# One access pattern over both directions in the HGRN2 levels, and 24 modulation vectors computed in halves inside attention: two-layer hybrid diffusion backbone

## The chip, the cores and the metric

The kernel runs on one core of one Trainium2 chip. The metric is the device time of one execution in microseconds (us). Engines are named as in the profile: PE is TensorE (PEld its weight loads), DVE is VectorE, ACT is ScalarE, POOL is GpSimd, SP is SyncE, whose queue issues the DMAs.

## The reference

One inference step of two post-norm layers over 1152 tokens (1024 latent, 128 context) of width 1024, all in float32. In each layer the stream is scaled and shifted by modulation vectors, `mod = silu(cvec) @ w_mod + b_mod` (6 x 1024 columns, for two condition vectors), projected once, and split among three mixers: latent attention with 8 heads, a bidirectional mLSTM, and a bidirectional gated linear recurrence (HGRN2). Their outputs are joined, projected, gated and normalised; a modulated SwiGLU FFN follows. The part of the recurrence that matters here, per direction, with `lb` the layer's lower bound (zero in layer 0):

```python
def decay(fr):
    f = lb + (1.0 - lb) * jax.nn.sigmoid(fr)
    return (1.0 - lb) * jax.nn.sigmoid(-fr), jnp.log(jnp.maximum(f, TINY))
...
Bc = jnp.cumsum(gc, axis=2)
decay = jnp.exp(Bc[:, :, :, None, :] - Bc[:, :, None, :, :])
A = jnp.einsum('bhtsc,bhsc->bhts', qc[:, :, :, None, :] * decay, kc)
```

## The kernel before

Products of float32 precision are made of three matmuls on pairs of rounded high and low parts (`mm3`, L153). The code is written in program order; a list scheduler that works at build time orders each engine's instructions by their dependencies and this order, so the order on the chip is not that of the source, and an engine works through its queue strictly in the order that was fixed.

Each layer has four phases. Phase A (`phase_a`, L367) computes the projections for HGRN2 and the mLSTM, and the inputs of attention, which it spills to memory. HGRN2 goes in two halves p of two heads each: `project` (three units: two gates, query), then the column group gi, during which `prep` (L521) turns the gates into cumulative logarithms, then the groups ckv and cq in `mla_prep` (L883), then `states` and, for each of three blocks b of 384 tokens, `outs` (L588). `outs` builds the token-by-token matrix A of three chunks of 128 tokens: a diagonal product, evicted by DVE with a multiplication by the identity (L600), and seven levels with block sizes m = 64 to 1. A level takes four differences on POOL (L610 to L613, forward and backward halves apart, 192 columns each), one exponential on ACT, three products on DVE (L615 to L617), six matmuls, and two masked copies by DVE into A (L624). L645 copies the output of a chunk. There are 2 layers x 2 halves x 3 blocks x 7 = 84 levels. The mLSTM (`mlstm`, L811) ends phase A; in layer 0 its normalising products run on POOL, in layer 1 on DVE (`LG`, L816).

Phase B is attention (`phase_b`, L965). After the projections of head 0 it goes through 152 steps (8 heads x 19 blocks of keys and queries). A step issues the score matmuls, the exponential on ACT (L1185), its rounding on ACT (L1186), the subtraction that gives the low part on POOL (L1187), and the product with the values of the step two before. Into the steps generators are mixed, two pieces per step: the maxima of the next head's scores (L1136 on PE, L1137 on DVE), projections of later heads, and at the end `rec` (L1222), which gates the recurrent outputs. DVE's other work from two SBUF tiles there is L1108, L151 and the copies of L1128. Phase C is the output projection with the first normalisation, phase D the FFN.

Of the 48 x 128 modulation columns layer 0 needs sixteen blocks ("vectors") at the start; the others are computed beside other work by `mod_gemv` (L209): a load of 512 KB and two dot products on DVE (L213), one per condition vector. Vectors 16 to 23 run in gi, ckv and cq, 24 to 39 in the mLSTM (`start_mod`, L282: two load buffers, its own copies cB of the conditions), 40 to 47 in the FFN's input, and those of layer 1 in the FFN's output (L1620), three per token tile of its first two passes. `gsave` (L222) transposes the gate vectors on PE and stores them. A branch for vectors in attention exists (L1283 to L1292) but starts at 40 and does nothing.

## Time and profile before

| | us |
|---|---|
| median of 3 runs | 3641.23 (3634.70 to 3644.34) |
| the profiled execution | 3641.28 |
| its span, first to last instruction | 3639.5 |
| mean granted clock of TensorE | 0.953 of 2.4 GHz |

Layer 0 runs from 0 to about 1795 us: phase A to about 560, attention's steps from 614.6 to 933.3, the FFN's output from 1542. Layer 1 fills the rest, attention's steps from 2394.6 to 2707.8. Busy time of PE is modelled and overstates its rate; stages are best compared by the times between like instructions of the two layers, which do the same work but for the vectors and the place of `LG`.

### The profile page before, as it was taken

How to read it: one execution, taken by the hardware profiler on the slowest of the kernel's cores; microseconds unless marked ns; L12 is line 12 of the kernel's file. 1: busy time of each engine (PE TensorE's matmuls, PEld its weight loads, DVE VectorE, ACT ScalarE, POOL GpSimd, SP SyncE). 2: the span in 40 equal slices, each digit the busy share in tenths (PEclk: the TensorE clock that was granted, in tenths of full speed). 3: DMA queues.
4: the chain of work that ended last, by engine and by line, in shares of the span. 5: the costliest groups of instructions: out<-in, count | busy, mean ns of one | idle time of the engine just before them, and what ended most of it. 6: DMA issues, size and time to landing. Idle time of an engine off the chain costs nothing. (4 is left out here: it accounts for less than half of the span.)

```text
span 3639.5 us, 56085 instructions
## 1 busy us (share of the span) xinstructions
PE 3405.9 (94%) x20556; PEld 3034.6 (83%) x20556; DVE 2264.8 (62%) x4492; ACT 1635.7 (45%) x2877; POOL 1988.8 (55%) x1745
## 2 busy tenths in 40 slices
PE   7999987999989999999889989989999999999997
PEld 7998875776779999988689888877767899998875
DVE  6868878555674444487775678765558544443246
ACT  4264564887343333312272636577853433333211
POOL 3455566777665555401453556567863555552176
PEclk9899976999989999999999999789999999999998
DMA  6212153002352222375422021401044322224222
GB/s 244 72 40 43 39 167 100 18 21 81 121 160 85 85 85 85 111 252 179 156 79 62 30 45 34 137 25 25 22 132 139 110 73 73 73 74 139 94 99 80
DMA packets 331272, 335.77 MB, mean 92 GB/s; under 512 B 191458, under 2 KB 270386, under 8 KB 330996
## 3 DMA queue, kind: packets, MB, share of 16 engines
q1 hardware_dynamic: 330996, 332.19, 29.5%
q8 instruction: 161, 2.64, 0.3%
q14 instruction: 115, 0.94, 0.1%
HBM read 263.54 MB, written 68.56 MB: 91 GB/s over the span
## 5 line engine op out<-in xcount | busy, mean ns | idle before, releaser
L151 POOL TENSOR_TENSOR t<-t,t 128x512 fp32r<-128x512 f32 (+3 forms) x318 | 437.8, 1378 | 374.8 <-ACT t L150 374.4
L150 ACT CAST t<-t 128x512 fp32r<-128x512 f32 (+5 forms) x404 | 270.7, 673 | 698.0 <-PE bank L1449 278.7
L1449 PE MATMUL bank<-hhi,t 128*128 128x256 f32 (+1 forms) x2816 | 570.8, 295 | 12.4 <-DVE t L1349 11.5
L155 PE MATMUL bank<-hhi,t 128*128 128x384 f32 (+1 forms) x1220 | 455.1, 378 | 19.2 <-ACT t L150 5.1
L157 PE MATMUL bank<-hhi,t 128*128 128x384 f32 (+1 forms) x1220 | 460.0, 378 | 8.8 <-DVE t L151 8.8
L1449 PEld LDWEIGHTS bank<-hhi,t 128*128 128x128 f32 x2816 | 456.2, 189 | 13.6 <-ACT t L150 12.3
L156 PE MATMUL bank<-hlo,t 128*128 128x384 f32 (+1 forms) x1220 | 460.9, 378 | 4.9 <-POOL hlo L151 4.1
L1187 POOL TENSOR_TENSOR t<-t,t 128x512 fp32r<-128x512 f32 (+1 forms) x304 | 383.3, 1281 | 125.4 <-ACT t L1186 103.0
L1449 PE MATMUL bank<-t,t 128*128 128x320 f32 (+1 forms) x3168 | 434.2, 297 | 2.3 <-DVE t L1507 1.7
L1449 PEld LDWEIGHTS bank<-t,t 128*128 128x128 f32 x3168 | 427.9, 190 | 3.7 <-DVE t L1507 1.9
L1449 PE MATMUL bank<-hlo,t 128*128 128x320 f32 (+1 forms) x1408 | 415.2, 295 | 0.0
L155 PE MATMUL bank<-t,hhi 128*128 128x256 f32 (+3 forms) x1232 | 386.8, 315 | 12.1 <-DVE t L1107 5.4
L156 PE MATMUL bank<-t,hhi 128*128 128x256 f32 (+3 forms) x1232 | 388.0, 315 | 4.3 <-POOL t L146 4.3
L157 PE MATMUL bank<-t,hlo 128*128 128x256 f32 (+3 forms) x1232 | 388.4, 316 | 0.3 <-POOL hlo L151 0.3
L155 PEld LDWEIGHTS bank<-hhi,t 128*128 128x128 f32 x1220 | 237.9, 196 | 57.3 <-ACT t L150 6.7
L1137 DVE TENSOR_REDUCE t<-bank 128x1 f32<-128x384 f32 (+1 forms) x400 | 203.9, 538 | 122.6 <-PE bank L1136 119.5
L157 PEld LDWEIGHTS bank<-hhi,t 128*128 128x128 f32 x1220 | 240.1, 197 | 39.2 <-DVE t L151 12.1
L156 PEld LDWEIGHTS bank<-hlo,t 128*128 128x128 f32 x1220 | 239.6, 196 | 34.7 <-POOL hlo L151 5.1
L1449 PEld LDWEIGHTS bank<-hlo,t 128*128 128x128 f32 x1408 | 265.4, 188 | 0.3 <-issue 0.2
L155 PEld LDWEIGHTS bank<-t,hhi 128*128 128x128 f32 x1232 | 239.8, 195 | 30.2 <-DVE t L1107 5.6
L213 DVE SCALAR_TENSOR_TENSOR t<-t,t 128x1024 bf16<-128x1024 f32 x176 | 239.3, 1359 | 40.6 <-DMA t<-in_w_mod_dram 31.6
L156 PEld LDWEIGHTS bank<-t,hhi 128*128 128x128 f32 x1232 | 240.4, 195 | 20.1 <-POOL t L146 4.7
(355 smaller groups left out, 7329.1 us busy)
## 6 DMA issues: line engine op xcount, KB each, us to landing
t<-in_w_mod_dram SPq DMA_DIRECT2D x96, 512.0 KB
t<-in_w_ffn_in_dram SPq DMA_DIRECT2D x88, 512.0 KB
t<-in_w_ffn_out_dram SPq DMA_DIRECT2D x44, 512.0 KB
t<-in_w_in_dram SPq DMA_DIRECT2D x40, 512.0 KB
shid<-t SPq DMA_DIRECT2D x88, 160.0 KB
sx<-t SPq DMA_DIRECT2D x27, 512.0 KB
t<-sx SPq DMA_DIRECT2D x27, 512.0 KB
shid<-t SPq DMA_DIRECT2D x88, 128.0 KB
```

Source lines behind the costliest of these rows:

```text
L150: self.nc.scalar.copy(hi, src)
L151: (eng or self.nc.gpsimd).tensor_tensor(lo, src, hi.bitcast(F32), op=ALU.subtract)
L155: mm(ps, a[0], b[0], start=first, stop=False)
L156: mm(ps, a[0], b[1], start=False, stop=False)
L157: mm(ps, a[1], b[0], start=False, stop=last)
L213: nc.vector.scalar_tensor_tensor(junk, raw, 1.0, cB[s], op0=ALU.mult, op1=ALU.mult, accum_out=self.modfm[:, l, j, s:s + 1])
L1137: V.tensor_reduce(nm[:, i, b:b + 1] if i < 8 else nm[:, i, 3:4], ps, axis=AX.X, op=ALU.max, negate=True)
L1187: G.tensor_tensor(pl, e, ph.bitcast(F32), op=ALU.subtract)
L1449: mm(ps, a[x][:, k * P:(k + 1) * P], view(y, k, n0, n1), start=first and k == 0 and i == 0, stop=k == 3 and i == 2, skip_group_check=True)
```

## The change

1. The five buffers of an HGRN2 half become two, `kq` (forward keys, backward keys, queries) and `bb` (both cumulative logarithms), so that one pattern reaches forward and backward halves: a level takes two POOL differences and two DVE products of 384 columns.
2. The diagonal product comes after the levels, by a masked copy with the identity as mask. The coarsest level is copied whole by ACT; the finer levels and the diagonal overwrite what does not belong to it.
3. `prep` leaves out the scaling by 1 - lb and the bound in layer 0, where lb is zero.
4. `start_mod` is gone. Vectors 16 to 39 are computed in layer 0's attention, one dot at three of every seven steps, with one load buffer `rv`; `cB` is loaded at the first step, and the buffers of `rec` lie in its storage.

```diff
+        def tiles(z):
+            kq, bb = z([P, 3, T]), z([P, 2, T])
+            return [kq[:, 2], kq[:, 0], kq[:, 1], bb[:, 0], bb[:, 1], kq, bb]
+
+        def halves(a, off, sh, nb, m, bcast=False):
+            return bass.AP(tensor=a.tensor, offset=a.offset + off, ap=[list(a.ap[0]), [2 * m, nb], [sh, 2], [0 if bcast else 1, m]])
...
-                    V.tensor_scalar(k[:, c], k[:, c], oml[:, p:p + 1], None, op0=ALU.mult)
-                    V.tensor_scalar(s, B[:, c], oml[:, p:p + 1], lb[:, p:p + 1], op0=ALU.mult, op1=ALU.add)
-                    V.tensor_scalar(s, s, TINY, None, op0=ALU.max)
+                    if l == 0:
+                        V.tensor_scalar(s, B[:, c], TINY, None, op0=ALU.max)
+                    else:
...
-                G.tensor_tensor(XS[:, :, 0, :], rf, F[:, :, 0, :], op=ALU.subtract)
-                G.tensor_tensor(XS[:, :, 1, :], rb, Bk[:, :, 1, :], op=ALU.subtract)
-                G.tensor_tensor(XM[:, :, 1, :], F[:, :, 1, :], rf, op=ALU.subtract)
-                G.tensor_tensor(XM[:, :, 0, :], Bk[:, :, 0, :], rb, op=ALU.subtract)
+                G.tensor_tensor(XS, halves(bb, o + m - 1, T + 1, nb, m, True), halves(bb, o, T + m, nb, m), op=ALU.subtract)
+                G.tensor_tensor(XM, halves(bb, o + T, m - T, nb, m), halves(bb, o + T + m, -T - 1, nb, m, True), op=ALU.subtract)
                 nc.scalar.activation(X, X, AF.Exp)
-                V.tensor_tensor(XS[:, :, 0, :], XS[:, :, 0, :], vw(kf[:, c])[:, :, 0, :], op=ALU.mult)
-                V.tensor_tensor(XS[:, :, 1, :], XS[:, :, 1, :], vw(kb[:, c])[:, :, 1, :], op=ALU.mult)
+                V.tensor_tensor(XS, XS, halves(kq, o, T + m, nb, m), op=ALU.mult)
                 V.tensor_tensor(X[:, 1, :], X[:, 1, :], q[:, c], op=ALU.mult)
+                product(X[:, 0], X[:, 1], (lambda o, ps: nc.scalar.copy(o, ps)) if li == 0 else pick(lmask[:, li, :]))
+            X = rX.next()
+            nc.gpsimd.tensor_tensor(X[:, 0, :], kf[:, c], kb[:, c], op=ALU.add)
+            product(X[:, 0], q[:, c], pick(imask))
...
-                        bg = self.start_mod(Zone(self, c, "gemv"), 16, 24) if l == 0 else iter(())
+                        bg = iter(())
...
-                bg = self.start_mod(zl, 24, 40) if l == 0 else iter(())
+                bg = iter(())
...
-            rdn = z.ring(2, [1, QB])
-            rr, rg = z.ring(3, [P, 256]), z.ring(3, [P, 256])
+            dn = z([33, QB])
+            rdn = Ring([dn[0:1, :], dn[32:33, :]])
+            cB = [z([P, D]) for _ in range(2)]
+            rr, rg = [Ring([a[:, 256 * i:256 * (i + 1)] for i in range(4)]) for a in cB]
+            if l == 0:
+                rv = z([P, U])
...
-            todo, gj = [], [40]
+            todo, mods = [], [(j, i) for j in range(16, 40) for i in range(2)]
...
+                if l == 0 and n == 0:
                     self.mod_init(cB)
+                if l == 0 and n % 7 in (0, 2, 4) and mods:
+                    j, i = mods.pop(0)
+                    if i == 0:
+                        nc.sync.dma_start(rv, ins["w_mod"][0, j])
+                    self.mod_dot(0, j, i, cB, rv, junk)
+                    if i == 1 and j % 8 == 7:
                         self.mod_bias(0, j - 7, 8)
+                    if (j, i) == (23, 1):
+                        self.gsave(0, 16, r_p.next())
```

`product` is the six matmuls and two evictions of a level as before, `pick` the masked copy, `mod_dot` one dot of `mod_gemv`.

## Rows read from the trace of the kernel before

**Rows 1.** The page, part 1: busy us, share of the span, instructions, by engine.
```profile
PE 3405.9 (94%) x20556; PEld 3034.6 (83%) x20556; DVE 2264.8 (62%) x4492; ACT 1635.7 (45%) x2877; POOL 1988.8 (55%) x1745
```

**Rows 2.** One line's instructions, layer 0, then 1: ns min/median/max; first, last start; forms.
```profile
L399 DVE TENSOR_TENSOR t<-bank,t x9: 392/413/415, 96.6 to 125.9; 128x256 f32<-128x256 f32 x9
...
L949 DVE TENSOR_TENSOR t<-bank,t x9: 393/416/425, 164.2 to 186.9; 128x256 f32<-128x256 f32 x9
...
L645 ACT COPY t<-bank x18: 247/266/281, 239.9 to 481.4; 128x128 f32<-128x128 f32 x18
...
L1185 ACT ACTIVATE t<-bank x152: 267/598/621, 614.6 to 926.8; 128x512 f32<-128x512 f32 x144, 128x128 f32<-128x128 f32 x8
...
L399 DVE TENSOR_TENSOR t<-bank,t x9: 400/425/425, 1910.0 to 1927.9; 128x256 f32<-128x256 f32 x9
...
L949 DVE TENSOR_TENSOR t<-bank,t x9: 391/417/419, 1959.8 to 1983.1; 128x256 f32<-128x256 f32 x9
...
L645 ACT COPY t<-bank x18: 247/266/279, 2040.0 to 2287.3; 128x128 f32<-128x128 f32 x18
...
L1185 ACT ACTIVATE t<-bank x152: 269/598/644, 2394.6 to 2702.0; 128x512 f32<-128x512 f32 x144, 128x128 f32<-128x128 f32 x8
```

**Rows 3.** Windows: length; busy us of PE, PEld, DVE, ACT, POOL; PEclk, DMA share, GB/s.
```profile
96.00:164.00 68.00, 62.06 (x478) 60.80 (x478) 59.65 (x171) 21.40 (x33) 33.47 (x31) 0.89 0.18 56
150.00:330.00 180.00, 178.76 (x1322) 168.06 (x1322) 135.28 (x362) 88.05 (x121) 96.95 (x122) 1.00 0.14 43
481.00:615.00 134.00, 96.23 (x456) 80.84 (x455) 121.14 (x329) 53.76 (x122) 94.86 (x96) 0.68 0.50 157
1985.00:2140.00 155.00, 145.19 (x1023) 135.12 (x1021) 107.97 (x257) 87.55 (x116) 83.28 (x111) 0.98 0.12 37
2287.00:2395.00 108.00, 90.40 (x457) 79.86 (x457) 91.32 (x294) 59.93 (x145) 55.10 (x65) 0.68 0.41 122
```

**Rows 4.** Line 213, the modulation dots, in 90 to 615 us: columns as rows 2.
```profile
L213 DVE SCALAR_TENSOR_TENSOR t<-t,t x44: 1198/1216/2010, 90.0 to 607.7; 128x1024 bf16<-128x1024 f32 x44
```

**Rows 5.** Lines of the HGRN part, whole span: columns as rows 2.
```profile
L593 POOL TENSOR_TENSOR t<-t,t x12: 1004/1020/1907, 83.6 to 2232.3; 128x384 f32<-128x384 f32 x12
...
L610 POOL TENSOR_TENSOR t<-t x84: 501/510/2485, 96.4 to 2272.7; 128x192 f32<-128x192 f32 x84
...
L615 DVE TENSOR_TENSOR t<-t,t x84: 293/359/2272, 107.5 to 2279.6; 128x192 f32<-128x192 f32 x84
...
L617 DVE TENSOR_TENSOR t<-t,t x84: 533/551/2724, 108.1 to 2280.2; 128x384 f32<-128x384 f32 x84
...
L527 DVE TENSOR_SCALAR t<-t,t x24: 405/420/2496, 79.4 to 2035.3; 128x384 f32<-128x384 f32 x24
```

**Rows 6.** Timeline 1110 to 1116 us, DVE, then POOL: start us, us, instruction, idle before.
```profile
1111.87 1.23 DVE L213 SCALAR_TENSOR_TENSOR t<-t,t 128x1024 bf16<-128x1024 f32 x1 [2.94 <-DMA t<-in_w_mod_dram]
...
1113.13 2.19 DVE L213 SCALAR_TENSOR_TENSOR t<-t,t 128x1024 bf16<-128x1024 f32 x1
...
1109.57 1.29 POOL L151 TENSOR_TENSOR t<-t,t 128x512 fp32r<-128x512 f32 x1 [1.20 <-ACT t L150]
1112.69 1.55 POOL L151 TENSOR_TENSOR t<-t,t 128x512 fp32r<-128x512 f32 x1 [1.83 <-ACT t L150]
```

**Rows 7.** Window of layer 0's first 109 attention steps: columns as rows 3.
```profile
614.00:841.00 227.00, 221.05 (x1075) 173.55 (x1075) 125.73 (x249) 186.58 (x364) 167.64 (x138) 0.98 0.08 17
```

**Rows 8.** Groups on DVE in 614 to 841: count, busy us, mean ns, idle before.
```profile
L1128 DVE CAST t<-hlo 32x1152 fp32r<-32x1152 f32 x5 | 6.8, 1355 | 1.0 <-PE bank L1182 0.8
L1108 DVE TENSOR_TENSOR t<-t,t 128x384 f32<-128x384 f32 x3 | 5.8, 1934 | 0.0
L151 DVE TENSOR_TENSOR t<-t,t 64x1152 fp32r<-64x1152 f32 x3 | 5.3, 1765 | 1.2 <-ACT t L150 1.1
```

**Rows 9.** Line 1611, evictions of the FFN output's first pass, layer 0, then 1.
```profile
L1611 ACT COPY t<-bank x18: 571/584/592, 1563.6 to 1662.8; 128x512 f32<-128x512 f32 x18
...
L1611 ACT COPY t<-bank x18: 572/586/589, 3340.5 to 3439.8; 128x512 f32<-128x512 f32 x18
```

More of the change, by code (lines that the diff above doesn't have):

```diff
@@ L390, in phase_a @@
                     zs = Zone(self, c0, f"hs{l}", "right")
-                    set0 = [zs([P, T]) for _ in range(5)]
+                    set0 = g.tiles(zs)
                     self.mark(f"hg{l}")
@@ L407, in phase_a @@
                     zt = Zone(self, cH, f"ht{l}")
-                    set1 = [zt([P, T]) for _ in range(5)]
+                    set1 = g.tiles(zt)
                     g.states(0, set0, v, rW)
@@ L487, in evac_unit @@
         def evac_unit(p, j, tiles):
-            q, kf, kb, Bf, Bb = tiles
+            q, kf, kb, Bf, Bb, kq, bb = tiles
             u = 3 * p + j
@@ L521, in prep @@
         def prep(p, tiles, rW):
-            q, kf, kb, Bf, Bb = tiles
+            q, kf, kb, Bf, Bb, kq, bb = tiles
             for b in range(NB):
@@ L539, in states @@
         def states(p, tiles, v, rW):
-            q, kf, kb, Bf, Bb = tiles
+            q, kf, kb, Bf, Bb, kq, bb = tiles
             V.memset(Sall[:, 0, 0, :], 0.0)
@@ L661, in hgrn_setup @@
             pass
+        G.tiles = tiles
         G.project, G.project_unit, G.prep, G.states, G.outs = project, project_unit, prep, states, outs
@@ L978, in phase_b @@
             vs[0], qT[2] = ze([P, 10, 130], F32R), pair(ze, [97, T])
-            ze([P, 576])
+            junk = ze([P, 576]).bitcast(BF16)[:, 0:D]
             kTs[0], kC[0], kC[2] = pair(ze, [97, T]), pair(ze, [97, P]), pair(ze, [97, P])
```

72 lines of the change are left out of this document (23 added, 49 removed).

## The prediction, made before the change was run

> **What bounds the kernel now.** I read the totals first: TensorE is busy 94% of the span, VectorE 62%, GpSimd 55% [rows 1]. A change that takes work off VectorE and GpSimd can therefore only give back time in stretches where TensorE stands still for them. So I looked for those stretches by laying the two layers side by side: both run the same stages, but only layer 0 computes its own 24 modulation vectors (48 dot products on VectorE) in between.
>
> The first and last starts of four instructions mark the stages [rows 2]. From the first eviction of the group gi to the first eviction of cq layer 0 takes 164.2 - 96.6 = 67.6 us, layer 1 1959.8 - 1910.0 = 49.8 us: 17.8 us more in layer 0. From the last HGRN output copy to the first attention exponential (the mLSTM, then the projections of head 0) layer 0 takes 614.6 - 481.4 = 133.2 us, layer 1 2394.6 - 2287.3 = 107.3 us: 25.9 us more. Between the two, from the first eviction of cq to the last output copy, layer 0 is even faster (317.2 against 327.5 us).
>
> The stage windows say why. In 96 to 164 VectorE is busy 59.65 of 68 us, and TensorE's mean granted clock is 0.89 of 2.4 GHz; in 481 to 615 VectorE is busy 121.14 of 134 us, GpSimd 94.86, TensorE 96.23. The same stage of layer 1 has VectorE at 91.32 of 108 us and GpSimd at 55.10 [rows 3]. The dots are the surplus: 44 of the 48 run between 90 and 615, 1.216 us each at the median, up to 2.010 us [rows 4]. In the HGRN stretches TensorE lacks 1.2 us of 180 in layer 0 and 9.8 us of 155 in layer 1 [rows 3]: little to win there.
>
> **The change part by part.**
>
> *The vectors leave phase A.* The first eight go from the stretch of gi and ckv, where VectorE was the late engine: without some 12 dots x 1.216 = 15 us there (the first ones run before 96), and without two of three scalings in preparing each block and direction (6 blocks and directions per half x 2 x about 0.42 us [rows 5] = 5 us), VectorE needs about 40 of the 68 us, and TensorE's own pace is next. I take 16 of the 17.8 us. The other sixteen (32 dots, 39 us at the median) leave the mLSTM stage. The next to be late there is GpSimd: layer 0 keeps on it the normalising products that layer 1 gives to VectorE, hence 94.86 against 55.10 us, part of it waiting behind dots. So I take 22 of the 25.9 us. Bounds: 5 to 18 us and 10 to 26 us, the upper ends being all that layer 0 takes longer (GpSimd's 94.86 us would leave 39 us of room in 134, so it does not forbid this). Sum: -38 us, bounds -15 and -44.
>
> *Their loads.* 24 loads of 512 KB leave SP's queue in phase A, and one of the two broadcasts of the two condition rows goes. In attention they share one buffer, so SP waits for the second half of a vector before it can load the next, and VectorE waits for the load. Behind SP's wait stand the small transfers of the softmax denominators, which no matmul needs before the output projection. Behind VectorE's wait stand the maxima of the score blocks, and TensorE needs their banks. A dot that waited for its load shows 2.94 us [rows 6]; two or three attention steps of 312.2 / 151 = 2.07 us [rows 2] lie between a vector and the next, so I charge nothing, and at most 24 x 2.94 = 71 us of VectorE time, which its idle 101 us in this window would still hold [rows 7].
>
> *The dots in attention.* 48 halves at three in seven steps take about 109 steps, 226 us: the window 614 to 841. VectorE is busy 125.73 us in it, so 48 x 1.216 = 58.4 us would fit. But GpSimd is busy 167.64 us there, and ScalarE 186.58 [rows 7]. And dots and GpSimd instructions keep each other out: at 1111.87 a dot that starts with GpSimd idle takes 1.23 us, and the next, which starts 0.44 us into a GpSimd subtraction, takes 2.19 us; the subtraction itself, begun under the first dot, takes 1.55 us where the one three microseconds before took 1.29 us [rows 6]. So the two engines' times add. VectorE's other work from two tiles in SBUF and its long casts there take 6.8 + 5.8 + 5.3 = 17.9 us [rows 8]. Together 167.6 + 17.9 = 185.5 of 227 us are taken (82%), and with the dots 243.9 us. That is over the window by 17 us if every microsecond of it were used. Some of these durations already hold such waiting: the three sums of rotated halves, 384 columns from two tiles, average 1.934 us [rows 8] where a product of that size takes 0.551 [rows 5]. That is 4 us for these three, by estimate 10 us in all, so that 234 us are needed; but no stretch uses every microsecond, and 234 / 0.95 = 246. I take +18 us. Bounds: 0, by the nearest stage that takes vectors beside matmuls without cost (the first pass of the FFN's output: from its first to its last eviction 99.2 us with 27 vectors in layer 0, 99.3 us without any in layer 1 [rows 9]), and +58 us, see the first rival.
>
> The Trainium skill (SBUF — State Buffer, section "SBUF: two separate sides") states that the pair of SBUF ports which VectorE and GpSimd share is locked by whichever instruction starts first, a VectorE instruction with two SBUF inputs among them, and that the other is blocked for the whole instruction. By that rule, which the 2.19 us agree with, the sum is the one above; without it the dots would fit into VectorE's idle time and the result would be 18 us lower.
>
> *The bank of the gate transpose.* One transpose of finished gates and its store move from phase A into attention, where they take one of the three projection banks once: nothing, at most a microsecond or two.
>
> *The levels of the recurrence* (84 of them, both layers). GpSimd: four subtractions of 192 columns at about 0.51 us become two of 384 at 1.02 us, the price of the addition of that size [rows 5]: no saving in its time, two instructions fewer. The new pattern has one axis more, which no row shows; the nearest bound it by 384 / 512 of the 1.29 us of a long subtraction, 0.97 us, and by the 1.55 us of one held up by a dot [rows 6]. I take 1.02, since 0.51 us is the median over all block sizes and the least is 0.501. VectorE: two products of 0.359 us become one of 0.551 us: -0.17 us x 84 = -14 us. Per output block 16 evictions on VectorE become 14; the two of the coarsest level go to ScalarE at under 0.584 us, its price for 512 columns [rows 9], 24 in all. Since TensorE lacks so little in these stretches, I take -3 us for both layers. The diagonal product, now last in a block, costs nothing as long as the projections' matmuls run beside it, as they do now; without them its addition and eviction would stand at the end of 12 blocks, 12 x (1.02 + 0.58) = 19 us. Bounds: -11 (all that TensorE lacks) and +19.
>
> **The sum.** -38 + 18 - 3 = -23 us. The profiled execution took 3641.28 us, 1.8 us more than its span of 3639.5 us, and equals the median of the runs (3641.23), so the forecast is 3618 us.
>
> **The rivals.**
> 1. *Slower: the shared path chokes attention.* One mechanism: dots and GpSimd's subtractions of the exponentials exclude each other in steps 0 to 109 of layer 0, the subtraction comes late, the third product of the step waits, and TensorE with it. For it: the 185.5 of 227 us taken already, and ScalarE at 82% beside it. Against it: two steps of lag between a subtraction and its product. If this path can be used no better than now (82%), the window becomes 234 / 0.82 = 285 us, +58 us; the result is 3641 - 41 + 58 = 3658 us. It decides from +41 us on, where the gain of phase A is eaten up: a window of 268 us, a path used below 87%. Chance 0.15. The Trainium skill's page named above (SBUF — State Buffer) is the rule that points this way.
> 2. *Attention is free.* Dots slip into VectorE's idle 101 us as they do in the FFN: 3600 us. For it: [rows 9]; against it: GpSimd's 74% in this window. Chance 0.2.
> 3. *The vectors were cover for something else.* In the mLSTM stage GpSimd's chain takes their place at once and only some 15 us come back, attention takes 18: 3641 - 15 - 3 + 18 = 3641 us, no change. For it: GpSimd's 94.86 of 134 us; against it: layer 1. Chance 0.17.
> 4. *The merged pattern is dear on GpSimd* (1.55 us): 84 x 2 x 0.53 = 89 us more on an engine that is about half idle in these stretches (96.95 of 180 us busy [rows 3]); by estimate a quarter shows, 22 us: 3641 - 38 + 18 + 22 = 3643 us. Chance 0.04.
>
> The forecast itself, between 3608 and 3632, has the remaining 0.44.
>
> **The numbers.** What a measurement of this kernel can tell from no change is about 0.3%, 11 us: below 3630 is faster, above 3652 slower. Faster: 0.44 of the forecast and 0.2 of rival 2, nearly all: 0.63. Same: rivals 3 and 4 and a little of the rest: 0.22. Slower: 0.15. The range runs from 3591 (rival 2 with phase A's upper bound and half of the levels': 3641 - 44 - 6) to 3655 (rival 1 nearly at its price).
>
> **What would show it.** Right: no dot before 614 in layer 0; the span from the last output copy to the first exponential near 111 us and that from gi to cq near 52 us; the first 109 attention steps of layer 0 near 245 us, GpSimd busy nearly throughout, dots with a mean well above 1.3 us. Wrong: the mLSTM stage of layer 0 above 125 us (rival 3), the 109 steps under 232 us (rival 2) or over 265 us (rival 1); GpSimd's level subtractions over 1.3 us (rival 4); or a layer 1 that moves by more than 10 us, for which I have no reason.

## The result, and the profile after

The changed kernel takes 3675.89 us (median of 4 runs, 3672.14 to 3683.26) against 3642.78 us of the kernel before on the same chip: a ratio of 1.0094, 95% interval 1.0078 to 1.0111. It is slower; the forecast was 3618 us. The profiled execution of after took 3683.26 us (span 3681.5), 42.0 us more than that of before.

The totals of the page of after, which answer to [rows 1]: VectorE, ScalarE and GpSimd hardly move, although GpSimd has 168 instructions fewer, and TensorE does the same 20556 instructions in 34 us more.

```profile
PE 3440.0 (93%) x20556; PEld 3055.8 (83%) x20556; DVE 2276.4 (62%) x4362; ACT 1625.8 (44%) x2882; POOL 1963.5 (53%) x1577
```

The same four markers as in [rows 2], in the trace of after (L386 is gi, L942 cq, L637 the output copy, L1182 the exponential of the scores), layer 0 first:

```profile
L386 DVE TENSOR_TENSOR t<-bank,t x9: 393/409/424, 82.4 to 104.1; 128x256 f32<-128x256 f32 x9
L942 DVE TENSOR_TENSOR t<-bank,t x9: 393/415/425, 136.1 to 158.6; 128x256 f32<-128x256 f32 x9
L637 ACT COPY t<-bank x18: 259/267/289, 217.1 to 470.7; 128x128 f32<-128x128 f32 x18
L1182 ACT ACTIVATE t<-bank x152: 271/598/627, 590.2 to 937.7; 128x512 f32<-128x512 f32 x144, 128x128 f32<-128x128 f32 x8
...
L386 DVE TENSOR_TENSOR t<-bank,t x9: 410/425/425, 1930.1 to 1949.4; 128x256 f32<-128x256 f32 x9
L942 DVE TENSOR_TENSOR t<-bank,t x9: 393/417/421, 1981.3 to 2004.7; 128x256 f32<-128x256 f32 x9
L637 ACT COPY t<-bank x18: 247/267/284, 2060.8 to 2313.1; 128x128 f32<-128x128 f32 x18
L1182 ACT ACTIVATE t<-bank x152: 268/598/618, 2430.3 to 2744.5; 128x512 f32<-128x512 f32 x144, 128x128 f32<-128x128 f32 x8
```

From them, and from the same markers in the traces of the experiments, come the stage lengths in us. "Front" is the way to the first cq (in layer 1 from the last eviction of layer 0's FFN output), "HGRN" from there to the last output copy, "mLSTM" from there to the first exponential, "attention" from the first to the last exponential. The unmerged kernel was profiled twice, and its stages agreed within 4 us. But e5, which runs the operations of before in the same time, has a stage 9.0 us shorter (HGRN of layer 1: 318.5), and the profiled executions of after and e2 are the slowest of theirs, 7 and 9 us above the median: a few microseconds in one stage tell nothing.

| kernel | layer 0: front | HGRN | mLSTM | attention | layer 1: front | HGRN | mLSTM | attention |
|---|---|---|---|---|---|---|---|---|
| before | 164.2 | 317.2 | 133.2 | 312.2 | 107.6 | 327.5 | 107.3 | 307.4 |
| after | 136.1 | 334.7 | 119.5 | 347.5 | 113.8 | 331.8 | 117.2 | 314.2 |
| vectors alone (e1) | 136.8 | 322.2 | 117.2 | 348.4 | 107.5 | 329.6 | 110.0 | 314.3 |
| levels alone (e2) | 162.2 | 323.5 | 120.7 | 307.6 | 112.4 | 330.5 | 114.0 | 315.4 |
| merged operations alone (e6) | 155.4 | 329.5 | 121.5 | 311.7 | 113.2 | 332.8 | 99.4 | 313.2 |
| order alone (e7) | 165.6 | 312.1 | 129.7 | 317.4 | 108.7 | 312.0 | 110.2 | 307.7 |
| after, levels unmerged (e14) | 138.3 | 304.4 | 112.1 | 343.5 | 108.6 | 311.5 | 111.2 | 306.1 |
| after, projections held (e13) | 136.1 | 320.8 | 121.7 | 341.7 | 113.7 | 323.5 | 116.4 | 316.7 |

So the vectors gave back 28.1 us in the front and 13.7 in the mLSTM stage of layer 0 and cost 35.3 in its attention. That is -6.5 us. The other 48.5 us are HGRN in layer 0 (+17.5) and layer 1, which has no vectors at all: +20.4 us up to its first exponential and +6.8 in attention (the rest, 3.8, lies in the stages between). The +6.8 cannot be put down to the levels: e1, which leaves them alone, has +6.9 there.

Windows of after by stage, columns as [rows 3]; 590:845 answers to [rows 7], and 471:531 and 2313:2373 are the first 60 us of the mLSTM stages:

```profile
82.00:136.00 54.00, 51.59 (x455) 51.04 (x455) 39.80 (x136) 16.70 (x28) 29.17 (x27) 1.00 0.18 53
217.00:471.00 254.00, 243.96 (x1738) 225.26 (x1737) 184.62 (x410) 129.20 (x199) 128.23 (x121) 0.96 0.18 46
471.00:531.00 60.00, 54.34 (x210) 47.29 (x210) 37.66 (x140) 28.70 (x87) 39.76 (x56) 0.50 0.49 148
471.00:590.00 119.00, 94.21 (x392) 80.53 (x391) 87.75 (x263) 49.78 (x127) 75.95 (x97) 0.59 0.39 123
590.00:845.00 255.00, 233.91 (x1056) 174.97 (x1056) 187.19 (x333) 185.12 (x358) 192.02 (x135) 0.93 0.20 60
2061.00:2313.00 252.00, 240.24 (x1731) 221.98 (x1730) 184.11 (x410) 131.75 (x198) 126.36 (x121) 0.97 0.17 42
2313.00:2373.00 60.00, 50.74 (x198) 44.38 (x198) 42.39 (x137) 30.93 (x94) 25.98 (x32) 0.54 0.51 150
```

The matching windows of before, those that [rows 3] and [rows 7] do not hold: from first to last output copy, and the first 60 us of the mLSTM stage, in both layers; last the same 109 steps of attention:

```profile
240.00:481.00 241.00, 231.87 (x1659) 213.43 (x1659) 186.34 (x442) 132.51 (x207) 139.52 (x182) 0.96 0.19 48
481.00:541.00 60.00, 48.43 (x272) 42.03 (x271) 53.06 (x150) 32.66 (x81) 39.78 (x44) 0.72 0.65 197
2040.00:2287.00 247.00, 231.70 (x1670) 213.79 (x1670) 183.84 (x450) 127.89 (x188) 134.91 (x180) 0.97 0.16 40
2287.00:2347.00 60.00, 54.51 (x289) 49.81 (x289) 45.79 (x155) 39.57 (x104) 30.11 (x38) 0.66 0.54 159
615.00:836.00 221.00, 215.05 (x1050) 168.97 (x1048) 122.38 (x242) 182.35 (x357) 163.56 (x135) 0.98 0.08 17
```

Three things are to be seen. *The outputs are TensorE's stretch in both kernels*: it lacks 9 and 15 us there before, 10 and 12 after, but after it runs 79 and 61 matmuls more. *The mLSTM stage has them less, and its clock falls*: in its first 60 us TensorE does 210 matmuls instead of 272, and 198 instead of 289, at 0.50 and 0.54 of 2.4 GHz instead of 0.72 and 0.66. In 471:531 it is busy 54 of 60 us, so it hardly waits; it works at the lower level, 1.2 GHz. *Attention was TensorE's as well*: 215 busy of 221 us before, at 0.98. After it idles 21 us instead of 6, and its busy time is 19 us more at 0.93.

The level instructions themselves, in the trace of after (both subtractions, the product, the copy; columns as [rows 5]), and the dots from 300 to 960 us, which answer to [rows 4]:

```profile
L609 POOL TENSOR_TENSOR t<-t x84: 821/865/1482, 92.9 to 2295.6; 128x384 f32<-128x384 f32 x84
L610 POOL TENSOR_TENSOR t<-t x84: 823/910/1330, 94.3 to 2296.4; 128x384 f32<-128x384 f32 x84
L612 DVE TENSOR_TENSOR t<-t,t x84: 543/559/2752, 96.1 to 2302.0; 128x384 f32<-128x384 f32 x84
L614 ACT COPY t<-bank x24: 459/482/514, 157.5 to 2274.9; 128x384 f32<-128x384 f32 x24
...
L216 DVE SCALAR_TENSOR_TENSOR t<-t,t x48: 1182/1362/4703, 542.3 to 748.7; 128x1024 bf16<-128x1024 f32 x48
```

None of them is dear. A pair of merged subtractions takes 1.78 us where the four took 2.14 (medians 0.51, 0.51, 0.57 and 0.55; the prediction took 0.51 for all). Ten of the 48 dots still start before the first exponential (from 542.3 us on, against 590.2), so attention holds 38.

### The profile page after: what moved, and what is told of

It is laid out like the page before. It is cut to its first block, busy times and chain, and to the rows that moved or that the text cites. A ratio compares the mean times of both kernels' runs of the same rounds, so it can differ in the third digit from the quotient of the medians.

```text
span 3681.5 us, 55802 instructions
## 1 busy us (share of the span) xinstructions
PE 3440.0 (93%) x20556; PEld 3055.8 (83%) x20556; DVE 2276.4 (62%) x4362; ACT 1625.8 (44%) x2882; POOL 1963.5 (53%) x1577
## 5 line engine op out<-in xcount | busy, mean ns | idle before, releaser
L1184 POOL TENSOR_TENSOR t<-t,t 128x512 fp32r<-128x512 f32 (+1 forms) x304 | 407.2, 1360 | 150.3 <-ACT t L1183 122.1
L155 PE MATMUL bank<-hhi,t 128*128 128x384 f32 (+1 forms) x1220 | 453.9, 378 | 25.8 <-DVE t L1104 7.1
L155 PE MATMUL bank<-t,hhi 128*128 128x256 f32 (+3 forms) x1232 | 384.5, 313 | 16.3 <-DVE t L1104 8.0
L155 PEld LDWEIGHTS bank<-hhi,t 128*128 128x128 f32 x1220 | 237.8, 196 | 60.0 <-DVE t L1104 9.3
L216 DVE SCALAR_TENSOR_TENSOR t<-t,t 128x1024 bf16<-128x1024 f32 x176 | 252.6, 1435 | 50.0 <-DMA t<-in_w_mod_dram 47.4
L155 PEld LDWEIGHTS bank<-t,hhi 128*128 128x128 f32 x1232 | 237.5, 193 | 34.3 <-DVE t L1104 8.1
L157 PEld LDWEIGHTS bank<-t,hlo 128*128 128x128 f32 x1232 | 238.4, 194 | 15.4 <-issue 0.2
```

Source lines behind the costliest of these rows:

```text
L155: mm(ps, a[0], b[0], start=first, stop=False)
L157: mm(ps, a[1], b[0], start=False, stop=last)
L216: self.nc.vector.scalar_tensor_tensor(junk, raw, 1.0, cB[s], op0=ALU.mult, op1=ALU.mult, accum_out=self.modfm[:, l, j, s:s + 1])
L1184: G.tensor_tensor(pl, e, ph.bitcast(F32), op=ALU.subtract)
```

## The experiments

### Which part lost: e1 and e2

The two halves of the change alone, each on the kernel before: e1 has the part on the vectors and attention's buffers, e2 the one on the recurrence.

```diff
# e1
-                bg = self.start_mod(zl, 24, 40) if l == 0 else iter(())
+                bg = iter(())
...
+                if l == 0 and n % 7 in (0, 2, 4) and mods:
# e2
+                G.tensor_tensor(XS, halves(bb, o + m - 1, T + 1, nb, m, True), halves(bb, o, T + m, nb, m), op=ALU.subtract)
...
+            product(X[:, 0], q[:, c], pick(imask))
```

> The kernel before with the part on the 24 vectors alone: no vectors in the front stretch and the mLSTM stage, all 48 halves in layer 0's attention with one load buffer; the levels stay as they were. Theory A (the levels are what lost, in both layers; the vectors were about even): the front stretch and the mLSTM stage of layer 0 give back some 28 us together, as in the whole change (gi to cq 67.6 to 53.7, last outs to first score 133.2 to 119.5), attention of layer 0 from first score to last av goes from 319 to about 350, layer 1 does not move (start and end of its attention within 5 us of before, relative to its start), time 3635 to 3652, within 0.3% of before. Theory B (the vectors lost, through attention and through the new layout of attention's buffers, which both layers share): layer 1 is longer by some 25 us here too, time 3665 to 3685.

> The kernel before with the part on the recurrence alone: merged subtractions and product, the coarsest level copied by ScalarE, the diagonal product last, no lower bound in layer 0; the vectors stay in the front, the mLSTM stage and attention as they were. Theory A: cq to last outs of layer 0 goes from 317 to about 335, layer 1 is longer by some 25 us between its start and its first score, time 3670 to 3690 (slower by 0.8 to 1.3%). Theory B: the recurrence is worth what was forecast, minus 11 to 0 us, time 3628 to 3643, and layer 1 does not move.

Measured: e1 3651.16 us, ratio 1.0025 (1.0008 to 1.0042); e2 3651.57 us, ratio 1.0030 (1.0017 to 1.0042). Neither theory holds as written. The vectors are about even, as A says (the table: front -27.4, mLSTM -16.0, attention +36.2), though layer 1 moves by 11.7 us from its first cq on, which A excluded; but the levels alone cost 8 us and not 27 to 47: layer 1 loses 14.5 us up to its first exponential and 8 in attention, while layer 0 wins 12.5 in the mLSTM stage. Alone the parts cost 7 and 8 us, together 33: they do not add.

### What attention lost: e3, e4, e8 and e9

e4 takes the waits for loads away, the others the second SBUF operand of the dots. e3, e8 and e9 differ in what ties the sum to its place.

```diff
# e3
-            self.nc.vector.scalar_tensor_tensor(junk, raw, 1.0, cB[s], op0=ALU.mult, op1=ALU.mult,
-                                            accum_out=self.modfm[:, l, j, s:s + 1])
+            self.nc.vector.tensor_reduce(self.modfm[:, l, j, s:s + 1], raw, axis=AX.X, op=ALU.add)
# e4
-                    if i == 0:
+                    if i == 0 and j == 16:
# e8
+                    V.tensor_tensor(rv[:, 0:1], rv[:, 0:1], cB[i][:, 0:1], op=ALU.mult)
+                    V.tensor_copy(junk[:, 0:1], rv[:, 0:1])
+                    V.tensor_tensor(rv[:, 0:1], rv[:, 0:1], junk[:, 0:1], op=ALU.add)
+                    V.tensor_reduce(self.modfm[:, 0, j, i:i + 1], rv, axis=AX.X, op=ALU.add)
# e9
+                    V.tensor_copy(junk[:, 0:1], cB[i][:, 0:1])
+                    V.tensor_copy(rv[:, 0:1], junk[:, 0:1])
+                    V.tensor_reduce(self.modfm[:, 0, j, i:i + 1], rv, axis=AX.X, op=ALU.add)
```

> The changed kernel with the dots of layer 0's attention made as a sum over the loaded row alone, so that VectorE reads one tensor of SBUF instead of two, as many instructions on as many elements. It leaves out the product with the condition. Theory A (what attention of layer 0 lost, 319 to 353 us, is that a two-input dot and GpSimd's instructions keep each other out): the sums take 1.1 to 1.3 us at all times, GpSimd's subtractions in layer 0 fall back from 1.54 to about 1.3 us, attention comes to 325 to 335. Theory B (the loss is VectorE's time and its queue: the dots stand ahead of evictions, whatever they read, and wait for loads): attention stays at 345 to 355 and the waits of the dots for their loads at some 47 us.

> The changed kernel with only the first of the 24 rows loaded: all 48 dots read that one row, so that no dot after the first waits for a load. It leaves out 23 loads, and so the right values of 23 vectors. Theory A (exclusion of dots and GpSimd, loads do not matter): attention of layer 0 stays within 6 us of 353. Theory B (one load buffer: the dot at the head of VectorE's queue waits for a load that is issued only when the dot before has ended, and evictions stand behind it): attention comes to 325 to 338.

> The changed kernel with each dot made as a sum over the loaded row alone, VectorE reading one tensor of SBUF where it read two, tied by three one-element operations to the condition's buffer and to the scratch buffer, so that the sums stand in layer 0's attention where the dots stood (in the earlier one-input kernel 30 of 48 had slipped ahead of the first score, so that it did not tell). It leaves out the product with the condition. Theory A (two-input dots and GpSimd's two-input instructions keep each other out): with over 30 sums between first and last score, GpSimd's subtraction takes 1.31 to 1.35 us against 1.51, a sum 1.2 us against the dot's 1.62, and first score to last av comes to 315 to 328 against 347.5. Theory B (it is VectorE's time and queue, whatever it reads): 340 to 352.

> The changed kernel with sums over the loaded row in place of the dots, as before, but tied to their place by two one-element copies that read one tensor each (the one-element operations of the run before read two tensors, took 0.46 and 0.57 us where a copy of one element took 0.15, and added some 1.2 us to each half). It leaves out the product with the condition. A half is then about 1.5 us of VectorE, the dot's 1.62. Theory A (a two-input operation of VectorE and GpSimd's instructions keep each other out, and that is the loss): GpSimd's subtraction 1.29 to 1.35 us, first score to last av of layer 0 315 to 328 us, TensorE's granted clock over these steps at 0.96 or more. Theory B (VectorE's time is the loss: the evictions that TensorE waits for stand behind 1.5 us of other work, whatever it reads, and TensorE's clock falls after the gaps): 335 to 355 us, clock 0.94 or less, although the subtraction takes 1.29 to 1.35 us.

Measured, attention of layer 0 as in the table: e4 350.6 us (3674.65 in all), so the loads and the single buffer are not the cause. e3 312.5 us (3652.76 in all), nothing lost; but with nothing tying them to the condition, 30 of its 48 sums ran ahead of the first exponential, so it tells only that 18 sums cost attention nothing. e8 tied them, and attention took 357.5 us (3670.73), longer than with dots: with the small operations meant to tie, a half took 2.39 us of VectorE against the dot's 1.62. Its groups on VectorE in 582 to 852, columns as [rows 8], show why:

```profile
L1289 DVE TENSOR_REDUCE modfm<-t 128x1 f32<-128x1024 f32 x42 | 51.1, 1216 | 1.1
L1286 DVE TENSOR_TENSOR t<-t,t 128x1 f32<-128x1 f32 x42 | 24.3, 578 | 18.1 <-DMA t<-in_w_mod_dram 17.8
L1288 DVE TENSOR_TENSOR t<-t,t 128x1 f32<-128x1 f32 x42 | 18.8, 448 | 0.9
L1287 DVE CAST t<-t 128x1 bf16<-128x1 f32 x42 | 6.3, 150 | 0.7
```

One element from two tiles takes 0.58 and 0.45 us, one from a single tile 0.15; a sum over 1024 columns takes its 1.2 us at all times, the dots 1.62 on average. Where GpSimd is idle as they start (41 of 96), the two-tile operations take 0.16 us at most; where it is at work, 0.50 and 0.63 at the median. So the exclusion is real. The Trainium skill (SBUF — State Buffer, section "SBUF: two separate sides") states it for VectorE instructions with two SBUF inputs against GpSimd instructions that read SBUF, and these rows agree.

e9 ties with copies that read one tile. The subtraction of the exponentials on GpSimd, groups in the steps 0 to 109, first before, then after, then e9:

```profile
L1187 POOL TENSOR_TENSOR t<-t,t 128x512 fp32r<-128x512 f32 x102 | 132.2, 1313 | 40.7 <-ACT t L1186 35.0 <-PE bank L1136 1.8 <-PE bank L1257 1.6
```
```profile
L1184 POOL TENSOR_TENSOR t<-t,t 128x512 fp32r<-128x512 f32 x102 | 151.7, 1509 | 53.9 <-ACT t L1183 45.7 <-PE bank L1254 5.3 <-PE bank L1181 3.0
```
```profile
L1184 POOL TENSOR_TENSOR t<-t,t 128x512 fp32r<-128x512 f32 x101 | 132.3, 1326 | 62.7 <-ACT t L1183 50.0 <-PE bank L1254 5.0 <-PE bank L1253 2.9
```

And e9's window of these steps, columns as [rows 7]:

```profile
582.00:830.00 248.00, 234.34 (x1052) 179.33 (x1052) 170.47 (x373) 184.03 (x357) 163.25 (x134) 0.91 0.21 59
```

The subtraction is back at 1.326 us, GpSimd is busy 163 us as before, and 40 sums stand between the scores, yet attention takes 337.1 us (3657.44 in all) at a clock of 0.91. Theory B's range holds. Of the 35.3 us, some 10 (347.5 - 337.1) go with the exclusion and some 25 (337.1 - 312.2) remain without it. In these steps TensorE had nothing to spare, and I read the remainder so: VectorE's extra 1.2 to 1.5 us now and then come between a bank and its eviction, TensorE idles a little, and its clock falls. That is argued from the windows and not shown; e3's 18 sums, which cost nothing, show that it is no plain price per sum. And as one execution each carries the split, its halves are good to several us only.

### Which part of the levels: e5, e6 and e7

The shared buffers alone; with them the merged operations, in the old order; and the new order alone, with four subtractions in separate buffers.

```diff
# e5
-                    set0 = [zs([P, T]) for _ in range(5)]
+                    set0 = g.tiles(zs)
# e6, with e5's line
-                G.tensor_tensor(XS[:, :, 0, :], rf, F[:, :, 0, :], op=ALU.subtract)
-                G.tensor_tensor(XS[:, :, 1, :], rb, Bk[:, :, 1, :], op=ALU.subtract)
+                G.tensor_tensor(XS, halves(bb, o + m - 1, T + 1, nb, m, True), halves(bb, o, T + m, nb, m), op=ALU.subtract)
...
# e7
+                product(X[:, 0], X[:, 1], (lambda o, ps: nc.scalar.copy(o, ps)) if li == 0 else pick(lmask[:, li, :]))
...
+            product(X[:, 0], q[:, c], pick(imask))
```

> The kernel before with one edit: the five tensors of a direction pair lie in two shared buffers (q with both k, and both B), all operations and their order as before. Theory A (the rewrite of the levels costs by its new order of work, with the diagonal product last): nothing moves, every stage within 3 us of before, time 3633 to 3655. Theory B (the shared buffers make operations wait that did not wait, first in the projection's evictions): layer 1's stretch from the end of layer 0 to the first gi goes from 57.7 to about 62, as it does in the levels-only kernel (61.7) and in the whole change (62.6), and cq to last outs of layer 1 grows by some 3 us.

> The kernel before with shared buffers, two subtractions and one product per level instead of four and two; the diagonal product still first and by a multiplication with the identity, the coarsest level still by a masked copy, the lower bound still applied in layer 0. Theory A (the order costs, the merged operations save): first to last outs of both layers falls by 2 to 6 us (241.5 and 247.3 before), time 3630 to 3643. Theory B (merging costs, since a merged subtraction waits for the scans of both directions and takes the buffer as one): first to last outs grows by 4 to 10 us a layer, as in the levels-only kernel (245.3 and 253.7), time 3645 to 3660.

> The kernel before with the order alone: the coarsest level first and copied by ScalarE, the diagonal product last with a masked copy; four subtractions and two products in separate buffers as before. Theory A: first to last outs grows by 4 to 10 us a layer and layer 1's way from last outs to first score by some 5 (107.3 before, 114.0 in the levels-only kernel), time 3648 to 3665. Theory B: within 4 us of before in these stages, time 3635 to 3650.

Measured: e5 3639.97 us, ratio 1.0002 (0.9989 to 1.0015), no change in time, although HGRN of layer 1 moved by more than A's 3 us. e6 3647.38 us, 1.0023 (1.0008 to 1.0037): from first to last output copy 251.0 and 249.5 us (before 241.5 and 247.3): theory B by its time and in layer 0, while layer 1 grew by only 2.2 us. e7 3627.79 us, 0.9968 (0.9954 to 0.9981): 233.0 and 231.1 us, faster by 8.5 and 16.2, and below both theories. My theory A, that the new order costs, was the wrong way round: the order gains and merging loses. Why the order gains is not shown.

### The levels unmerged in the changed kernel: e10 and e14

```diff
-                G.tensor_tensor(XS, halves(bb, o + m - 1, T + 1, nb, m, True), halves(bb, o, T + m, nb, m), op=ALU.subtract)
-                G.tensor_tensor(XM, halves(bb, o + T, m - T, nb, m), halves(bb, o + T + m, -T - 1, nb, m, True), op=ALU.subtract)
+                G.tensor_tensor(XS[:, :, 0, :], rf, F[:, :, 0, :], op=ALU.subtract)
+                G.tensor_tensor(XS[:, :, 1, :], rb, Bk[:, :, 1, :], op=ALU.subtract)
+                G.tensor_tensor(XM[:, :, 1, :], F[:, :, 1, :], rf, op=ALU.subtract)
+                G.tensor_tensor(XM[:, :, 0, :], Bk[:, :, 0, :], rb, op=ALU.subtract)
...
```

> The changed kernel with four subtractions and two products a level again; shared buffers, order, ScalarE's copy, prep and vectors as changed. Theory A (merging costs, by a longer stretch of outputs and by the gap it leaves at the entry of the mLSTM stage, after which TensorE's clock stays at its lower level): first to last outs of layer 1 falls from 252 to 230 to 240, TensorE's wait of 6.7 us at the entry of layer 1's mLSTM stage is under 3, and the time is 3645 to 3662. Theory B (the merged operations are not what costs; the order that the program was put in at build time moved by chance): the stretch stays at 246 to 255, time 3665 to 3685.

> The same kernel as the look with unmerged levels (3600.37), now timed. Theory A: its gain over before is real, 3593 to 3612 and faster than before by 0.8 to 1.3%. Theory B (a lucky execution): 3620 or more.

Measured: e10 3600.37 us; e14, the same program timed, 3603.41 us, ratio to before 0.9919 (0.9898 to 0.9939). It is faster than both kernels. Splitting the merged operations again is worth 72 us by the medians (3675.89 - 3603.41) and 64 by the ratios (1.0094 - 0.9919), more than either theory of e10 allowed and what theory A of e14 said. Most lies before attention: 37.7 us from cq to the first exponential in layer 0, 26.3 in layer 1. By the table 50.6 of these 64.0 us lie in the two HGRN stretches and only 13.4 in the mLSTM stages.

### Where the dots could go instead: e11 and e12

e11 puts all 24 vectors into the mLSTM stage of the kernel before; e12 adds e7's order and the missing lower bound.

```diff
-                bg = self.start_mod(zl, 24, 40) if l == 0 else iter(())
+                bg = self.start_mod(zl, 16, 40) if l == 0 else iter(())
...
-            for _ in range(2):
+            for _ in range(3):
                 next(bg, None)
```

> The kernel before with its 8 vectors of the front stretch moved into the mLSTM stage, three vectors a chunk there instead of two; attention and levels as before. Theory A (the front is VectorE's, the mLSTM stage has room, and attention has none): the front gives back what the vectors-only kernel gave there (to the first cq 164.2 to 137, to the first outs 5 of it back), the mLSTM stage goes from 133 to 135 to 145, attention of layer 0 stays at 312, time 3612 to 3632. Theory B (the mLSTM stage is bound by VectorE as well, at 1.7 us a dot as in the front): 133 to 155 or more, time 3636 to 3650.

> The kernel before with three parts: all 24 vectors in the mLSTM stage, the order of the change's levels (coarsest level first and copied by ScalarE, diagonal product last) with four subtractions and two products in separate buffers, and no lower bound in layer 0. Theory A (the parts add): the gain of the order alone (12.7) and that of the vectors in the mLSTM stage (10 to 30) together, 3600 to 3622, faster than both kernels. Theory B (TensorE bounds the stretch of the recurrence, so that what one part gives the next part's filler takes back): no more than the order alone gave, 3624 to 3640.

Measured: e11 3646.93 us, 1.0017 (1.0001 to 1.0034), theory B: the front falls by 27.7 us, the mLSTM stage rises to 150.7 and HGRN to 331.3. e12 3625.39 us, 0.9952 (0.9936 to 0.9967), theory B: the order's gain and little more. The mLSTM stage of layer 0 has no room for more vectors.

### What merging does: e13, e15 and e16

I looked at the mLSTM stage first. A wait is the first thing to be seen at the entry of layer 1's mLSTM stage. TensorE's longest wait in 2296 to 2356 of after (waited for: us in total, times, longest):

```profile
PE bank L845 <- DVE t L834: 6.7, 1, 6.7
```

Behind it, from the timelines of GpSimd and VectorE of after: a mask on GpSimd that waits for the load of the first chunk's decays, and the product on VectorE that waits for the mask.

```profile
2318.14 1.23 POOL L827 TENSOR_SCALAR_AFFINE_SELECT t<-t 128x512 f32<-128x512 f32 x2 [6.73 <-DMA t<-snr]
...
2320.45 0.76 DVE L834 TENSOR_TENSOR t<-bank,t 128x256 f32<-128x256 f32 x2 [4.37 <-POOL t L827]
```

Before, the longest wait there is 1.8 us, since projections still fill TensorE. They can be counted by one of the three matmuls of `mm3` (L155). Windows for that line alone, in the first 60 us of both mLSTM stages (length; busy us of PE and PEld; clock, DMA share, GB/s): after, before, the unmerged kernel e14, and e13.

```profile
471.00:531.00 60.00, 1.35 (x2) 0.62 (x2) 0.50 0.49 148
2313.00:2373.00 60.00, 1.19 (x2) 0.66 (x2) 0.54 0.51 150
```
```profile
481.00:541.00 60.00, 7.34 (x21) 4.73 (x20) 0.72 0.65 197
2287.00:2347.00 60.00, 6.81 (x20) 4.33 (x20) 0.66 0.54 159
```
```profile
443.00:503.00 60.00, 13.02 (x43) 8.01 (x43) 1.00 0.59 176
2252.00:2312.00 60.00, 6.92 (x22) 4.38 (x22) 0.60 0.54 159
```
```profile
457.00:517.00 60.00, 14.25 (x48) 9.28 (x48) 0.96 0.52 157
2289.00:2349.00 60.00, 15.82 (x48) 10.27 (x48) 0.88 0.51 149
```

With 2 projections the clock is 0.50 and 0.54, with about 20 it is 0.60 to 0.72, with 43 to 48 it is 0.88 to 1.00; e16, below, has 0.64 with 4. The program is put in order at build time, and there it is plain what moves: behind the last output copy's matmuls 192 projection matmuls of all kinds are left in each layer of after, 247 and 236 before, 269 and 243 in e14. e13 keeps the merged levels and holds projections back; e15 has e14's four subtractions with the merged product, e16 the merged subtractions with two products.

```diff
# e13
+        if name == "gg":
+            nc.vector.tensor_tensor(br[:, 0:1], br[:, 0:1], self.held, op=ALU.add)
...
+            if (p, b) == (1, NB - 1):
+                V.tensor_scalar(self.held, o[:, 2, 127:128], 0.0, None, op0=ALU.mult)
# e16
-                V.tensor_tensor(XS, XS, halves(kq, o, T + m, nb, m), op=ALU.mult)
+                V.tensor_tensor(XS[:, :, 0, :], XS[:, :, 0, :], vw(kf[:, c])[:, :, 0, :], op=ALU.mult)
+                V.tensor_tensor(XS[:, :, 1, :], XS[:, :, 1, :], vw(kb[:, c])[:, :, 1, :], op=ALU.mult)
```

> The changed kernel, levels merged as changed, with one small addition: the evictions of the last projection (the one whose rows the last filler stores) wait for a one-element value that the last output block writes, so that in the built order 300 instead of 192 projection matmuls stand behind the last output block of each layer (before: 247 and 236 by the same count, the unmerged kernel 269 and 243). Two one-element operations a layer are added, nothing is left out. Theory A (the merged levels drew the projections into the stretch of outputs; the mLSTM stage then has an entry gap and no dense work, and TensorE's clock stays at its lower level through it): granted clock of the mLSTM stage from 0.59 to 0.68 to 0.80 in both layers, cq to first score from 454 and 449 to 415 to 435, time 3610 to 3645. Theory B (the merged operations cost by themselves, or the clock of that stage is low whatever runs there): the two stretches stay at 440 or more and the time at 3660 to 3690, or longer where attention waits for the held rows.

> The changed kernel with four subtractions a level as before and the one product as changed; the built order leaves 241 and 258 projection matmuls behind the last output block. Theory A (the subtractions' merging alone moves the order, and the order the clock): mLSTM clock 0.68 or more in both layers, time 3595 to 3625. Theory B (the merged product is as much to blame): 3640 or more.

> The changed kernel with the two merged subtractions as changed and two products a level as before; the built order leaves 192 and 192 projection matmuls behind the last output block, as in the changed kernel. Theory A: mLSTM clock 0.56 to 0.63 in both layers as in the changed kernel, time 3660 to 3690. Theory B: 3640 or less.

Measured: e13 3656.32 us, ratio to before 1.0049 (1.0032 to 1.0066), so 16 us (by the ratios) to 20 us (by the medians) less than after. The mean clock of the whole mLSTM stage rises as theory A said, from 0.59 to 0.77 in layer 0 and 0.76 in layer 1. But cq to the first exponential falls only to 442.5 and 439.9 us, which is B's 440 and not A's 435, and the time lies between the theories. The mLSTM stages take 121.7 and 116.4 us, hardly other than the 119.5 and 117.2 of after: their length does not follow their clock (in layer 1, e16 has 105.7 us at 0.59 and before 107.3 at 0.68). And the gap moves: the outputs, now without enough projections beside them, stand still at their end. Their windows in e13, to set against 217:471 and 2061:2313 of after: TensorE lacks 17 and 18 us where it lacked 10 and 12.

```profile
214.00:457.00 243.00, 225.70 (x1583) 208.45 (x1583) 180.28 (x399) 107.35 (x172) 121.02 (x111) 0.93 0.17 41
2044.00:2289.00 245.00, 227.38 (x1588) 209.02 (x1588) 181.65 (x409) 110.50 (x177) 118.06 (x111) 0.94 0.16 39
```

The same windows of e14, outputs and then mLSTM stages:

```profile
215.00:443.00 228.00, 219.90 (x1616) 203.30 (x1617) 181.42 (x430) 115.22 (x182) 137.38 (x179) 0.99 0.19 45
2016.00:2252.00 236.00, 225.60 (x1673) 209.76 (x1674) 186.48 (x441) 124.40 (x191) 136.99 (x181) 0.98 0.17 42
443.00:555.00 112.00, 81.84 (x515) 70.84 (x511) 96.65 (x282) 66.28 (x149) 85.26 (x103) 0.81 0.49 150
2252.00:2363.00 111.00, 96.63 (x464) 85.20 (x461) 89.98 (x293) 61.90 (x144) 55.74 (x65) 0.63 0.41 123
```

After runs 122 and 58 matmuls more than e14 in its outputs, TensorE is busy 24 and 15 us longer there, and the windows are 26 and 16 us longer. The mLSTM stage that has lost this work gets no shorter by it. e13 gives the work back, 33 and 85 matmuls fewer than e14 in its outputs, and these still take 243 and 245 us: something in the merged levels themselves holds them up.

e16 took 3671.74 us in one execution, as after: A holds, the merged subtractions are what draws the projections forward (4 and 2 of L155 in the first 60 us, at 0.64 and 0.54; clock of the whole stages 0.65 and 0.59, the first a little above A's range). e15 took 3632.20 us, inside neither theory's range: 24 and 32 projections in the first 60 us, clocks 0.62 and 0.73 in the two stages where A wanted 0.68. Unmerging the subtractions is worth about 44 us, the product on top of it some 29 more, in one execution each, though by itself (e16) the product is worth almost nothing. In layer 1, cq to the first exponential is as short in e15 (421.6 us) as in e14 (422.7): there it is the subtractions alone.

What a merged subtraction waits for is to be seen where the second half of the recurrence begins. In layer 0 of after no subtraction of a level runs between 283 and 336 us; the first one follows the scan that makes the forward logarithms of the half's third block:

```profile
281.84 1.18 POOL L610 TENSOR_TENSOR t<-t 128x384 f32<-128x384 f32 x1
...
332.96 0.96 DVE L533 TENSOR_TENSOR_SCAN t<-t,t 128x384 f32<-128x384 f32 x1
...
336.13 0.83 POOL L609 TENSOR_TENSOR t<-t 128x384 f32<-128x384 f32 x1
```

In e14 the half's first subtraction starts 50 us ahead of that scan:

```profile
279.75 0.63 POOL L614 TENSOR_TENSOR t<-t 128x192 f32<-128x192 f32 x1
...
329.39 2.42 DVE L533 TENSOR_TENSOR_SCAN t<-t,t 128x384 f32<-128x384 f32 x1
```

It is so in all eighteen traces and in all four halves of each: in the nine with merged subtractions the first of them starts 1.1 to 3.8 us after the end of the third block's forward scan, in the nine with four subtractions, e5 with the shared buffers among them, 12.8 to 52.1 us before it. The first block's subtraction needs none of the third block's values. But the pattern over both directions reaches in memory from the first block's forward columns to its backward ones and so passes over the forward columns of the later blocks; that the build makes it wait for all that lies between is my inference from these times. While the second half stands, TensorE goes on with projections (in 284:336 of after 88 of L155 and 36 matmuls of the levels, in 279:331 of e14 80 and 72); I take this to be what draws them ahead of the levels. At the last exponential of that half's first block after is 28.5 and 24.6 us behind e14, counted from the first cq, against 30.3 and 20.3 us over the whole HGRN stretches; e13, which leaves this wait in place, is still 21.9 and 24.3 us behind. No run takes the wait away alone; and what it costs depends on the work around it, since e6 has it too and lost only 0.23%.

## Why the prediction was wrong

- *"The vectors leave phase A", -38 us.* Right: -28.1 and -13.7 are -41.8. The parts were mis-sized. The front gave 28.1 and not 16, since I compared only gi to cq with layer 1 and charged nothing to the way before it (96.6 to 82.4 us). The mLSTM stage gave 13.7 and not 22, and alone (e1) 16.0; ten dots still ran in it, against my sign that none would run before attention.
- *"The dots in attention", +18 us.* The sign and the exclusion were right, the size was 35.3 us, inside the bounds. The step that failed is the list of engines: it asked whether VectorE, GpSimd and ScalarE had room and passed over TensorE, busy 221.05 of 227 us in the very row I quoted [rows 7]. e9 puts only some 10 us on the exclusion. The rest I read as VectorE's work in front of evictions for which a full TensorE waits, with a clock that falls from 0.98 to 0.93; that is not shown.
- *"Their loads", nothing.* Right: e4 without them takes as long.
- *"The levels", -3 us, bounds -11 to +19.* This step failed, and with it the forecast. Every duration in it held or came out cheaper: subtractions 0.865 and 0.910 us for 1.02, the product 0.559 for 0.551, the copy 0.482 for at most 0.584. But I priced the merged subtraction by its length and put its wait at nothing. The runs show that it starts only behind the third block's forward scan, so that the second half's first exponential comes 54.5 and 47.7 us later than in e14, counted from the first cq. I also took "TensorE lacks so little in these stretches" to mean that little could be lost. TensorE went on with projections meanwhile, and the mLSTM stage, which then had fewer, got no shorter by it. Against the same kernel unmerged this costs 64 to 72 us. That the merged operations cost this is shown by e14, and that it is mostly the subtractions by e15 and e16, in one execution each; that the late start is the way is read from the traces.
- *The diagonal product last*, up to +19: it gains. The order alone is 0.9968 of before.
- *Layer 1, "no reason" to move by 10 us.* It moved by 27.2 us up to the end of attention, 20.4 of them before its first exponential, where e14 takes back 31.5. That was the sign I had named for a wrong forecast, and it is the one that came.
- *The rivals.* The result is slower, as rival 1 had it (3658 us), but not by its mechanism: attention lost 35 us and not the 58 of its price. Rival 3 was wrong too; the mLSTM stage stayed under 125 us. That the two parts of the change do not add (7 and 8 us alone, 33 together) no rival had.

What stays open: what the late start costs by itself, since a merged subtraction without that wait was not run; why merging costs 7 us alone (e6) and 64 to 72 in the changed kernel; and how much of each difference between near neighbours (e14 and e15: 29 us for one product a level) is an accident of the order made at build time. That TensorE's clock in the mLSTM stage is not the whole is shown by e13, which raised it to 0.77 and 0.76 and gave back 16 to 20 us.

## What to carry to other kernels

Before instructions are merged, ask not only what the merged one takes but what it must wait for: one pattern over two regions can wait for whatever lies between them. Where one engine is full, ask also what work fills it and who needs that filler next: a stretch that stands still uses the filler up early. Before work is put "beside" a stage, look first at the engine that bounds it, here TensorE at 97%, and only then at the idle time of the engine that gets the work. And where a scheduler fixes the order at build time, time the parts of a change alone and together: here the change without its merged operations made the kernel 0.8% faster, with them 0.9% slower.

## What was not expected of the hardware

TensorE's granted clock stood at 0.50 over 60 us in which it was busy 54 (window 471:531 of after). In e14 the first 60 us of the same stage, as busy by the profile's modelled times but with 409 matmuls for 210, were granted 1.00, columns as [rows 3]:

```profile
443.00:503.00 60.00, 53.95 (x409) 48.89 (x405) 49.35 (x168) 47.51 (x112) 46.76 (x64) 1.00 0.59 176
```

The Trainium skill (TensorE: Matmul & The Clock Gate, section "What's actually happening") states that the lower level is the default and that activity releases it. The 1.00 agrees; in after TensorE was busy nearly throughout at the lower level, and why is not for these runs to tell. And a one-element instruction of VectorE that reads two tiles took 0.45 to 0.58 us on average in attention, three to four times a copy of one element, and no longer than that copy where GpSimd was idle.
